# Three of four column groups of y transposed by DMA instead of TensorE, and C's gates fetched right behind A's

## The chip, the cores and the metric

The kernel runs on one NeuronCore of one Trainium2 chip. The metric is the device time of one execution in microseconds (us). Before the change the median of three runs is 1486.85 us (1486.48 to 1486.9). Engines are named as in the profile: PE is TensorE, DVE is VectorE, ACT is ScalarE, POOL is GpSimd, SP is SyncE, which here only issues DMAs.

## The reference

One decoder layer with three token mixers side by side, on 512 tokens and 2048 channels in float32. What matters here is the end of it:

```python
ua = (ya * silu(za)) @ w_branch_a          # sliding-window attention, 768 wide
ub = (yb * silu(zb)) @ w_branch_b          # forgetting attention, 768 wide
uc = (yc * silu(zc)) @ w_branch_c          # attention into memory tokens, 512 wide
g = sigmoid(gate_logits.reshape(b, s, 3, 2048))
y = g[:, :, 0] * ua + g[:, :, 1] * ub + g[:, :, 2] * uc
return x + y @ w_out
```

`y` is computed with tokens on partitions. For `y @ w_out` it is needed with channels on partitions, so y is transposed.

## The kernel before, in words

**Precision.** Every float32 product runs as three matmuls of a high and a low part: high x high, low x high, high x low. So each weights tile takes an ACT cast to the high part (`ac.copy`) and a DVE subtraction that leaves the low part. `parts` does both; in the profile the casts are at L1000 and L1125, the subtractions at L1001 and L1128.

**The late stage.** After the attention and z stages the kernel computes the three merge gates (stored to DRAM as `gates`), then y, then the product with w_out. A list of units, `late.units`, holds the order. y is made in four column groups (cg 0 to 3) of 512 channels. Each group has three units of branch B, three of A and two of C (class `Branch`), each of 24 matmuls of 128x512. DVE multiplies a finished bank by its gate (L1393 for B, which starts y; L1396 for A and C). POOL adds A's result to y, DVE adds C's.

**The transpose.** When C's last block is done, `flip` transposes the group: two pairs, each of eight 128x128 PE transposes into two PSUM banks (`yt`, L1421). The product with w_out uses seven block products in place of eight (a Strassen-like scheme), so `out` copies the four quarters of a pair into the places 3 and 4 (`y3s`, `y4s`, ACT L1430), makes four sums on DVE (L1012, L1015), stores one half of the results to DRAM (`y_alpha`, SP L1438, groups 0 to 2) and splits the other half into high and low (`yhy`, `yly`). `plan_y` later loads `y_alpha` back (`ya`, L1408), from the end of group 3's B units on, and splits it (`xhy`, `xly`).

**Places.** `place(n, ...)` are nine 4 KB-per-partition buffers, reused under many names. y lives in 5 and 7. Gates rotate through a ring of four (0, 1, 2, 6), two tiles per branch and group, so C's gates take the tiles of B's, and A's of the next group take those of C.

**What sets the order.** PE, DVE, ACT and POOL execute in the order that the program writes. That order comes from a clock that advances by 0.5 for every three matmuls; `later(dt, f)` puts f's instructions into their engines' streams dt further on. So one unit of 24 matmuls is 4 on this clock. The order on SP's queue is set by the framework's scheduler. Every engine and SP's queue run in order: an instruction that waits holds up all behind it. Weights for a unit are asked for four units ahead (`load`) and split two units ahead (`split`).

Of the kernel before, what the change touches and what calls it, by code (L numbers as in the profile page):

```python
# [11 lines left out]

F32 = mybir.dt.float32
F32R = mybir.dt.float32r
AF = mybir.ActivationFunctionType
ALU = mybir.AluOpType
AX = mybir.AxisListType
# [2 lines left out]
P = 128  # L20
# [36 lines left out]
def tile_hybrid_block(ctx, tc, xT, x, memT, mem, ng, mng, w_in, b_forget, gqa, gka, sinks, gqb, gkb, gqc, gkc,  # L57
                      w_mem, w_a, w_b, w_c, w_out, relm, out):
    nc = tc.nc
    ve, ac, po, pe, sy = nc.vector, nc.scalar, nc.gpsimd, nc.tensor, nc.sync  # L60
# [7 lines left out]
    def f32(ap):  # L68
        return ap.bitcast(F32)
# [9 lines left out]
    def place(n, name, dtype=F32):  # L79

        return yp.tile([P, 2, S], dtype, tag=f"ys{n}", name=name)
# [47 lines left out]
    yad = nc.dram_tensor("y_alpha", (D // 2, 1024), F32, kind="Internal").ap()  # L129
# [12 lines left out]
    def later(dt, f):  # L142
        at_slot(clock[0] + dt, f)
# [41 lines left out]

    def w_tile(which, dtype=F32R):

# [34 lines left out]
    def bank(i, name):  # L222
        return ps.tile([P, 512], F32, tag=TAGS[i], name=name)

    class Stream:
# [8 lines left out]
        def add(self, name, segs, kind, act, nkt, evac, pre=None):  # L234
            banks = {}
            nu = nkt if kind == "mem" else nkt // UK
            for u in range(nu):
                self.units.append((name, segs, kind, act, evac, pre, u, nu, banks))
# [756 lines left out]
    def blocks(xs):  # L995

        return xs.rearrange("p k (t n) -> p (k t) n", t=2)

    def parts(hi, lo, src, dt=0.5):
        ac.copy(hi, src)  # L1000
        later(dt, lambda: ve.tensor_tensor(lo, src, f32(hi), op=ALU.subtract))  # L1001

    def x_tiles(u, name):
        ax[u] = tuple(cp.tile([P, 4, 256], F32R, tag=f"a{p}{u}", name=f"x{p}{name}{u}") for p in "hl")
        return ax[u]

    def y_tiles(u, name):
        ay[u] = tuple(gp[0].tile([P, 3, 256], F32R, tag=f"b{p}{u}", name=f"y{p}{name}{u}") for p in "hl")
        return ay[u]
# [4 lines left out]
    def sub(out, a, b):  # L1014
        ve.tensor_tensor(out, a, b, op=ALU.subtract)  # L1015
# [50 lines left out]
    late = Late()  # L1066
# [248 lines left out]
    y_acc = {}  # L1315
# [19 lines left out]
    class Branch:  # L1335
# [20 lines left out]
        def fetch_g(self):  # L1356
            br, w, npair, gi, base = BR[self.bi]
            for i in range(2):
                t = r_tile(f"g{br}")
                sy.dma_start(out=t, in_=gdr[gi][i * 2 * P:(i + 1) * 2 * P, self.cg * 512:(self.cg + 1) * 512]  # L1360
                             .rearrange("(b p) n -> p b n", p=P))
                self.g[2 * i], self.g[2 * i + 1] = t[:, 0, :], t[:, 1, :]

        def run(self):
            br, w, npair, gi, base = BR[self.bi]
            xh, xl = y_split[base + self.p]
            first, last = self.p == 0, self.p == npair - 1
            if first:
                self.banks["tags"] = tags = ((2, 3), (0, 1))[ucnt[0] % 2]
                for b in range(4):  # L1370
                    self.banks[b] = bank(tags[b // 2], f"u{br}{self.cg}_{b}")
                ucnt[0] += 1
            if self.p == npair - 2:
                later(1, self.fetch_g)
            count = [0]
            for b in range(4):
                c = slice(b * P, (b + 1) * P)
                for k in range(2):
                    for i, (x, wt) in enumerate(((xh, self.hi), (xl, self.hi), (xh, self.lo))):
                        mm(count, self.banks[b], x[:, k, c], wt[:, k, :], start=(first and k == 0 and i == 0),  # L1380
                           stop=(last and k == 1 and i == 2))
                if last:
                    self.evac(b)
            if self.cg == 3 and last and self.bi == 0:
                plan_y()

        def evac(self, b):
            o, g = self.banks[b], self.g[b]
            if self.bi == 0:
                if b % 2 == 0:  # L1390
                    y_acc["t"] = place(5 + b, f"y{self.cg}{b}")
                y_acc[b] = y_acc["t"][:, b % 2, :]
                ve.tensor_tensor(y_acc[b], o, g, op=ALU.mult)  # L1393
                return
            y = y_acc[b]
            ve.tensor_tensor(g, o, g, op=ALU.mult)  # L1396
            if self.bi == 1:
                po.tensor_tensor(y, y, g, op=ALU.add)  # L1398
                return
            later(1, lambda: add(y, y, g))  # L1400
            if b == 3:
                flip(self.cg, dict(y_acc), self.banks["tags"])

    def plan_y():

        def one(u):
            xs = blocks(place(3 + u % 2, f"ya{u}"))
            sy.dma_start(out=xs, in_=yad[u * P:(u + 1) * P, :].rearrange("p (k n) -> p k n", n=256))  # L1408
            later(5, lambda: parts(*x_tiles(u, "y"), xs, 1))
        for u in range(6):  # L1410
            later((1, 3, 8, 10, 15, 17)[u], lambda u=u: one(u))

    def flip(cg, y, tags):

        def pair(q):
            u = 2 * cg + q
            banks = []
            for j in range(2):
                yt = bank(tags[q if cg < 3 else 1], f"yt{u}_{j}")
                for b in range(4):  # L1420
                    pe.transpose(yt[:, b * P:(b + 1) * P], y[b][:, (2 * q + j) * P:(2 * q + j + 1) * P], ident)  # L1421
                banks.append(yt)
            later(0.5, lambda: out(u, banks))

        def out(u, banks):
            xa, xb = (blocks(place(i, f"y{i}s{u}")) for i in (3, 4))
            a, s1, s2, d = (xa[:, i, :] for i in range(4))
            s3, c, s4, b = (xb[:, i, :] for i in range(4))
            for dst, j, h in ((b, 0, 1), (d, 1, 1), (a, 0, 0), (c, 1, 0)):
                ac.copy(dst, banks[j][:, h * 256:(h + 1) * 256])  # L1430

            def sums():
                add(s1, b, d)
                sub(s2, s1, a)
                sub(s3, a, b)
                sub(s4, c, s2)
                if cg < 3:
                    sy.dma_start(out=yad[u * P:(u + 1) * P, :].rearrange("p (k n) -> p k n", n=256), in_=xa)  # L1438
                parts(*y_tiles(u, "y"), xb[:, 0:3, :], 1)
                if cg == 3:  # L1440
                    later(2, lambda: parts(*x_tiles(u, "y"), xa, 1))
            later(1.5, sums)
        later(5, lambda: pair(0))
        later(9 if cg < 3 else 10.5, lambda: pair(1))

    for cg in range(4):
        for bi, (br, w, npair, gi, base) in enumerate(BR):
            banks, g = {}, {}
            for p in range(npair):
                late.units.append(Branch(cg, bi, p, banks, g))  # L1450
    n_branch = len(late.units)


# [73 lines left out]
    k = n_p4  # L1527
# [52 lines left out]
```

## Time and profile before

| | |
|---|---|
| median of three runs | 1486.85 us |
| the profiled execution's own time | 1487.16 us |
| its span | 1485.3 us |
| PE busy | 1476.7 us (99%) |
| DVE busy | 1086.1 us (73%) |
| ACT busy | 715.2 us (48%) |
| PE transposes of y | 64, first at 1197.4 us, last at 1342.6 us |
| column groups start at | 1190.73 (second), 1281.41 us (fourth) |

The profile shows one execution. Busy time is summed per engine. A group's row gives its count, busy time, the mean of one, and the idle time before it with what ended it. "The chain of waits" follows the last instruction back to what released it, step by step. Timeline rows begin with the start and the duration. Names are tiles: `rawl` raw weights, `wa` to `we` their high and low parts, `uA`, `uB`, `uC` the branches' banks, `P` the banks of a w_out product.

### The profile page before, as it was taken

The numbers are of one execution on the slowest core, as the hardware profiler recorded it, in microseconds if no ns is written. First come the engines' busy times: TensorE is split into PE (matmuls) and PEld (weight loads), VectorE is DVE, ScalarE is ACT, GpSimd is POOL, SyncE is SP. The second block draws the span as 40 slices with busy tenths as digits, with TensorE's granted clock in tenths as the row PEclk, the third lists the DMA queues.
The fourth block names the chain that finished last, engine by engine and source line by source line (L and its number), as shares of the span: only waits on it lengthen the run. The fifth ranks groups of instructions, "written<-read, shape, count | busy, mean of one in ns | idle before, by whom it ended". The sixth has DMA issues, their size and how long they took to land.

```text
span 1485.3 us, 20413 instructions
## 1 busy us (share of the span) xinstructions
PE 1476.7 (99%) x7225; PEld 1276.2 (86%) x7225; DVE 1086.1 (73%) x1868; ACT 715.2 (48%) x1206; POOL 202.8 (14%) x239
## 2 busy tenths in 40 slices
PE   9999999999999999999999999999999999999998
PEld 9999999998888888888888888888888888888887
DVE  5385875775678665469878888888887555589997
ACT  5545654664467564555344444444355332245442
POOL 0121431331334432200000000000000100110000
PEclk9999999999999999999999999999999999999999
DMA  8774235333345223476667676767676856476684
GB/s 287 223 214 127 79 94 160 88 108 120 122 140 164 74 87 98 161 256 233 202 219 226 216 224 213 239 205 245 209 228 214 294 179 207 162 247 222 245 285 154
DMA packets 127278, 277.40 MB, mean 187 GB/s; under 512 B 14140, under 2 KB 53692, under 8 KB 127176
## 3 DMA queue, kind: packets, MB, share of 16 engines
q1 hardware_dynamic: 122136, 259.58, 54.6%
q10 hardware_dynamic: 5040, 16.53, 3.3%
q8 instruction: 56, 0.92, 0.3%
q14 instruction: 46, 0.38, 0.1%
HBM read 244.58 MB, written 31.48 MB: 186 GB/s over the span
## 4 chain that ended last, share of the span: by engine, by line
PE 94%; ACT 2%; DMA 2%; DVE 1%; issue 1%; POOL 0%; ACTq 0%; DVEq 0%; POOLq 0%; SPq 0%
PE P L1083 41%; PE z L300 10%; PE qA L300 5%; PE kB L300 5%; PE vB L300 5%; PE qB L300 4%; PE uA L1083 4%; PE uB L1083 3%; PE qC L300 3%; PE kvA L300 3%; PE uC L1083 3%; PE mem L300 1%; PE avB L633 1%; PE ptB L623 1%; DMA gB<-gates 1%; PE avA L700 1%
## 5 line engine op out<-in xcount | busy, mean ns | idle before, releaser
L214 DVE TENSOR_TENSOR wc<-wa,wb 128x512 fp32r<-128x512 f32 (+2 forms) x254 | 149.7, 628 | 73.2 <-ACT wb L211 65.2
L211 ACT CAST wb<-wa 128x512 fp32r<-128x512 f32 (+2 forms) x254 | 131.4, 566 | 143.8 <-PE z L300 34.3
L1125 ACT CAST wa<-rawl 128x1024 fp32r<-128x1024 f32 x85 | 89.5, 1052 | 207.4 <-DVE rawl L1015 166.2
L1015 DVE TENSOR_TENSOR rawl<-rawl 128x512 f32<-128x512 f32 x256 | 176.9, 692 | 5.7 <-DMA rawl<-in_w_out_dram 1.3
L1128 DVE TENSOR_TENSOR wc<-rawl,wa 128x1024 fp32r<-128x1024 f32 x85 | 105.0, 1235 | 51.9 <-ACT wa L1125 50.3
L1128 DVE TENSOR_TENSOR we<-rawl,wd 128x512 fp32r<-128x512 f32 (+1 forms) x128 | 122.1, 954 | 4.1 <-ACT wd L1125 0.5
L1398 POOL TENSOR_TENSOR y<-y,gA 128x512 f32<-128x512 f32 x16 | 27.2, 1731 | 674.9 <-DVE gA L1396 674.9
L1125 ACT CAST wd<-rawl 128x512 fp32r<-128x512 f32 (+1 forms) x128 | 106.9, 835 | 22.7 <-DVE rawl L1015 19.9
L300 PE MATMUL z<-ah,wb 128*128 128x512 f32 x256 | 101.8, 398 | 0.0
L300 PE MATMUL z<-ah,wc 128*128 128x512 f32 x256 | 99.9, 390 | 0.0
L300 PE MATMUL z<-al,wb 128*128 128x512 f32 x256 | 99.8, 390 | 0.0
L1125 ACT CAST wb<-rawl 128x1024 fp32r<-128x1024 f32 x43 | 45.3, 1053 | 87.7 <-DVE rawl L1015 67.5
L1083 PE MATMUL P<-wd,xhx 128*128 128x512 f32 x192 | 74.7, 389 | 0.0
L1083 PE MATMUL P<-wd,xlx 128*128 128x512 f32 x192 | 74.7, 389 | 0.0
L1083 PE MATMUL P<-we,xhx 128*128 128x512 f32 x192 | 74.7, 389 | 0.0
L1128 DVE TENSOR_TENSOR wb<-rawl,wb 128x1024 fp32r<-128x1024 f32 x43 | 52.6, 1222 | 25.7 <-ACT wb L1125 25.4
L1012 DVE TENSOR_TENSOR R<-P,R 128x512 f32<-128x512 f32 (+1 forms) x90 | 57.1, 674 | 6.6 <-PE P L1083 5.8
L300 PEld LDWEIGHTS z<-ah,wc 128*128 128x128 f32 x256 | 48.0, 188 | 10.3
L300 PEld LDWEIGHTS z<-ah,wb 128*128 128x128 f32 x256 | 48.1, 188 | 9.3 <-DVE zA L937 0.3
L300 PEld LDWEIGHTS z<-al,wb 128*128 128x128 f32 x256 | 48.2, 188 | 9.1
L579 POOL TENSOR_SCALAR pA<-pA,denA 128x256 f32<-128x256 f32 (+1 forms) x48 | 45.0, 954 | 78.2 <-DVE denA L578 78.2
L1083 PE MATMUL P<-wa,xhx 128*128 128x512 f32 x128 | 49.8, 389 | 0.0
(407 smaller groups left out, 4189.6 us busy)
## 6 DMA issues: line engine op xcount, KB each, us to landing
rawl<-in_w_in_dram SPq DMA_DIRECT2D x144, 512.0 KB, 4.4
rawl<-in_w_out_dram SPq DMA_DIRECT2D x48, 512.0 KB, 5.7
wa<-in_w_in_dram SPq DMA_DIRECT2D x63, 384.0 KB, 3.5
wa<-in_w_in_dram SPq DMA_DIRECT2D x64, 256.0 KB, 3.0
rawl<-in_w_in_dram SPq DMA_DIRECT2D x48, 256.0 KB, 4.1
gates<-R ACTq DMA_DIRECT2D x24, 512.0 KB, 7.2
wa<-in_w_in_dram SPq DMA_DIRECT2D x16, 512.0 KB, 3.6
wa<-in_w_mem_dram SPq DMA_DIRECT2D x16, 512.0 KB, 3.4
```

The source lines that it names most:

```text
L211: ac.copy(hi[:, :n], raw[:, i, :n])
L214: ve.tensor_sub(lo[:, :n], raw[:, i, :n], f32(hi[:, :n]))
L300: pe.matmul(pb, a, m, start=b in fresh, stop=last and not todo[b])
L579: engine.tensor_scalar(p, p, den[:, 4 + i:5 + i], None, op0=ALU.mult)
L623: pe.transpose(tb[:, c:c + P], p[:, off[i] + j * P:off[i] + (j + 1) * P], ident)
L633: pe.matmul(av[:, j * P:], v[:, j, hv, :], t[:, BOFF[j]:BOFF[j] + n], start=(j == 0 and w == 0), stop=(j == NT - 1 and w == 1))
L1012: ve.tensor_tensor(out, a, b, op=ALU.add)
L1015: ve.tensor_tensor(out, a, b, op=ALU.subtract)
L1083: pe.matmul(*args, **kw)
L1125: ac.copy(hi[:, :k, :], src)
L1128: return lambda: ve.tensor_tensor(lo[:, :k, :], src, f32(hi[:, :k, :]), op=ALU.subtract)
L1398: po.tensor_tensor(y, y, g, op=ALU.add)
```

## The change

For column groups 0, 1 and 2 the PE transposes go. `flip_dma` does this in their place:

- `halves(b)`: ACT copies each token block of y, seen as 16-bit integers, into the tile of C's gates (whose use is over), low and high 16-bit halves apart. Four copies a group, of 1024 elements per partition.
- `send(h)`: SP issues a DMA transpose of a whole gates tile (128 partitions x 2048 16-bit elements, 512 KB) into y's own place, 5 or 7. Two a group.
- `combine`: as `out` before, but the copies (ACT, L1480 in the new numbering) read the transposed halves from SBUF and weave them back into 32-bit numbers: 512 16-bit elements each in place of 256 32-bit ones. The pairs are put at 6.5 and 8.5 on the clock behind the group's end (before, the copies were at 5.5 and 9.5).

Group 3 keeps the PE transposes. C's gates are asked for two clock steps behind A's, in A's second unit, and no longer in C's first. `plan_y` swaps the places 3 and 4 of the tiles that it loads. The ring of gates is unchanged.

```diff
@@ fetch_g
                 t = r_tile(f"g{br}")
                 sy.dma_start(out=t, in_=gdr[gi][i * 2 * P:(i + 1) * 2 * P, self.cg * 512:(self.cg + 1) * 512]
                              .rearrange("(b p) n -> p b n", p=P))
+                self.g["t", i] = t
                 self.g[2 * i], self.g[2 * i + 1] = t[:, 0, :], t[:, 1, :]
@@ Branch.run
-            if self.p == npair - 2:
+
+            if self.bi < 2 and self.p == npair - 2:
                 later(1, self.fetch_g)
+                if self.bi == 1:
+                    later(2, self.follower.fetch_g)
@@ Branch.evac
             if b == 3:
-                flip(self.cg, dict(y_acc), self.banks["tags"])
+                if self.cg < 3:
+                    flip_dma(self.cg, dict(y_acc), dict(self.g))
+                else:
+                    flip(self.cg, dict(y_acc), self.banks["tags"])
@@ plan_y
-            xs = blocks(place(3 + u % 2, f"ya{u}"))
+            xs = blocks(place(4 - u % 2, f"ya{u}"))
@@ 
+    def combine(u, copy):
+
+        cg = u // 2
+        xa, xb = (blocks(place(i, f"y{i}s{u}")) for i in (3, 4))
+        a, s1, s2, d = (xa[:, i, :] for i in range(4))
+        s3, c, s4, b = (xb[:, i, :] for i in range(4))
+        for dst, j, h in ((b, 0, 1), (d, 1, 1), (a, 0, 0), (c, 1, 0)):
+            copy(dst, j, h)
+
+        def sums():
+            add(s1, b, d)
+            sub(s2, s1, a)
+            sub(s3, a, b)
+            sub(s4, c, s2)
+            if cg < 3:
+                sy.dma_start(out=yad[u * P:(u + 1) * P, :].rearrange("p (k n) -> p k n", n=256), in_=xa)
+            parts(*y_tiles(u, "y"), xb[:, 0:3, :], 1)
+            if cg == 3:
+                later(2, lambda: parts(*x_tiles(u, "y"), xa, 1))
+        later(1.5, sums)
+
@@ flip
-                yt = bank(tags[q if cg < 3 else 1], f"yt{u}_{j}")
+                yt = bank(tags[1], f"yt{u}_{j}")
...
-            later(0.5, lambda: out(u, banks))
+            later(0.5, lambda: combine(u, lambda dst, j, h: ac.copy(dst, banks[j][:, h * 256:(h + 1) * 256])))
         later(5, lambda: pair(0))
-        later(9 if cg < 3 else 10.5, lambda: pair(1))
+        later(10.5, lambda: pair(1))
+
+    def u16(ap):
+        return ap.bitcast(U16)
+
+    def flip_dma(cg, y, g):
+        back = {}
+
+        def halves(b):
+            t = u16(g["t", b // 2]).rearrange("p i (x n) -> p (i x) n", n=P).rearrange("p (e k b) n -> p e k b n", e=2, b=2)
+            ac.copy(t[:, :, :, b % 2, :], u16(y[b]).rearrange("p (k n e) -> p e k n", k=4, e=2))
+
+        def send(h):
+            t = u16(place(5 + 2 * h, f"yh{cg}{h}"))
+            sy.dma_start_transpose(out=t.rearrange("p i (x n) -> p (i x) n", n=P),
+                                   in_=u16(g["t", h]).rearrange("p i n -> p (i n)"))
+            back[h] = t.rearrange("p i (k n) -> p i k n", k=4)
+
+        for h in range(2):
+            for b in (2 * h, 2 * h + 1):
+                later(0.5 + 0.5 * b, lambda b=b: halves(b))
+            later(1.5 + h, lambda h=h: send(h))
+        for q in range(2):
+            later((6.5, 8.5)[q], lambda q=q: combine(2 * cg + q, lambda dst, j, h: ac.copy(
+                u16(dst).rearrange("p (n e) -> p e n", e=2), back[h][:, :, 2 * q + j, :])))
@@ 
+            if bi == 2:
+                late.units[-4].follower = late.units[-2]
```

How the instructions move. First ACT at the border from group 0 to group 1, before (`rawl113` is the weights of A's second unit of group 1, `yt` the banks of PE's transposes):

```order
L1000 CAST wb127_11118<-rawl111_11030 128x1024 [waits DMAHW2_49,DVE_49,PE_49]
L1000 CAST wd102_11158<-rawl112_11068 128x1024 [waits DMAHW5_49,DVE_49,PE_49]
L1430 COPY y4s0_11169<-yt0_0_11148 128x256 [waits PE_49]
L1430 COPY y3s0_11168<-yt0_1_11153 128x256 [waits PE_49]
L1430 COPY y3s0_11168<-yt0_0_11148 128x256
L1430 COPY y4s0_11169<-yt0_1_11153 128x256
L1000 CAST yhy0_11189<-y4s0_11169 128x768 [waits DVE_49]
L1000 CAST wa127_11217<-rawl113_11105 128x1024 [waits DMAHW6_49]
L1430 COPY y4s1_11226<-yt1_0_11207 128x256 [waits DVE_49,PE_49]
L1430 COPY y3s1_11225<-yt1_1_11212 128x256 [waits DMAHW3_49,PE_49]
L1430 COPY y3s1_11225<-yt1_0_11207 128x256
L1430 COPY y4s1_11226<-yt1_1_11212 128x256
```

After the change ACT's stream at the same place reads so (`gC` the gates' tiles that take the halves, `yh` the transposed ones):

```order
L1467 COPY gC_30_10980<-y02_10907 128x8x128
L1001 CAST wd102_11156<-rawl112_11068 128x1024 [waits DMAHW5_49,PE_49,Activation_49]
L1480 COPY y4s0_11174<-yh01_11137 128x2x256 [waits DMAHW1_49,Activation_49]
L1480 COPY y3s0_11173<-yh01_11137 128x2x256
L1480 COPY y3s0_11173<-yh00_11126 128x2x256 [waits DMAHW7_49]
L1480 COPY y4s0_11174<-yh00_11126 128x2x256
L1001 CAST yhy0_11193<-y4s0_11174 128x768 [waits DVE_49]
L1480 COPY y4s1_11202<-yh01_11137 128x2x256 [waits DVE_49]
L1480 COPY y3s1_11201<-yh01_11137 128x2x256 [waits DMAHW5_49]
L1480 COPY y3s1_11201<-yh00_11126 128x2x256
L1480 COPY y4s1_11202<-yh00_11126 128x2x256
L1001 CAST wa127_11211<-rawl113_11105 128x1024 [waits DMAHW6_49,PE_49]
```

The copies of halves have come in between the weights casts (the last one is the first row); the cast of `rawl113` stood between the two pairs and now stands behind the second. The four copies of a pair read `yh`, and the second copy of the second pair waits for a DMA, the store of what the first pair left in that place.

DVE at the same border, after the change (`wc127` is the low half of `rawl113`, `y10` the next group's y):

```order
L1013 TENSOR_TENSOR y3s0_11173<-y4s0_11174,y3s0_11173 128x256 [waits Activation_49]
L1016 TENSOR_TENSOR y3s0_11173<-y3s0_11173 128x256 [waits DVE_49,Activation_49]
L1016 TENSOR_TENSOR y4s0_11174<-y3s0_11173,y4s0_11174 128x256
L1016 TENSOR_TENSOR y4s0_11174<-y4s0_11174,y3s0_11173 128x256 [waits DVE_49,Activation_49]
L1002 TENSOR_TENSOR yly0_11194<-y4s0_11174,yhy0_11193 128x768 [waits Activation_49]
L1398 TENSOR_TENSOR y10_11214<-uB1_0_11107,gB_31_11159 128x512 [waits DMAHW3_49,DMAHW7_49,PE_49,Activation_49]
L1013 TENSOR_TENSOR y3s1_11201<-y4s1_11202,y3s1_11201 128x256 [waits DMAHW5_49]
L1016 TENSOR_TENSOR y3s1_11201<-y3s1_11201 128x256 [waits DVE_49]
L1016 TENSOR_TENSOR y4s1_11202<-y3s1_11201,y4s1_11202 128x256
L1016 TENSOR_TENSOR y4s1_11202<-y4s1_11202,y3s1_11201 128x256 [waits DVE_49]
L1002 TENSOR_TENSOR wc127_11212<-rawl113_11105,wa127_11211 128x1024 [waits DMAHW6_49,Activation_49]
```

Before, `wc127` stood directly behind the multiply that writes `y10`, ahead of the second pair's sums; now it is behind them. The multiply also waits for ACT now: `y10` lies where the transposed halves are read.

SP's queue at this border, before:

```order
L1342 DMA rawl113_11105<-in_w_a_dram 128x2x512 [waits DMAHW6_49,DMAHW1_49,DVE_49]
L1360 DMA gA_33_11305<-gates_0 128x2x512 [waits DVE_49]
L1360 DMA gA_34_11307<-gates_0 128x2x512 [waits DMAHW0_49,DVE_49]
L1342 DMA rawl114_11140<-in_w_a_dram 128x2x512 [waits DMAHW2_49,DVE_49]
L1342 DMA rawl115_11199<-in_w_c_dram 128x2x512 [waits DMAHW5_49,DVE_49]
L1438 DMA y_alpha<-y3s0_11168 128x1024 [waits DMAHW3_49,DVE_49]
L1342 DMA rawl116_11260<-in_w_c_dram 128x2x512 [waits DMAHW6_49,DMAHW4_49,DVE_49]
L1438 DMA y_alpha<-y3s1_11225 128x1024 [waits DVE_49]
```

and after:

```order
L1343 DMA rawl113_11105<-in_w_a_dram 128x2x512 [waits DMAHW6_49,DMAHW1_49,DVE_49]
L1471 DMA_TRANSPOSE yh00_11126<-gC_29_10978 128x16x128 [waits DVE_49,Activation_49]
L1343 DMA rawl114_11148<-in_w_a_dram 128x2x512 [waits DMAHW2_49,DMAHW0_49,DVE_49]
L1471 DMA_TRANSPOSE yh01_11137<-gC_30_10980 128x16x128 [waits Activation_49]
L1343 DMA rawl115_11196<-in_w_c_dram 128x2x512 [waits DMAHW5_49,DVE_49]
L1361 DMA gA_33_11293<-gates_0 128x2x512 [waits DMAHW7_49,DMAHW3_49]
L1361 DMA gA_34_11295<-gates_0 128x2x512 [waits DMAHW4_49,DMAHW1_49]
L1436 DMA y_alpha<-y3s0_11173 128x1024 [waits DVE_49]
L1436 DMA y_alpha<-y3s1_11201 128x1024 [waits DMAHW6_49,DVE_49,Activation_49]
L1343 DMA rawl116_11248<-in_w_c_dram 128x2x512 [waits DVE_49]
```

The next group's A gates have moved from ahead of one weights transfer to behind two, and behind both transposes; the two stores of `y_alpha` now stand together, ahead of the weights of C's second unit (`rawl116`). In group 3 the first request for `ya` (L1408, new L1416) stands for place 4 in place of 3, and the transfers of the second w_out unit (`rawl134`) stand behind `ya2` instead of ahead of it.

More of the change, by code (lines that the diff above doesn't have):

```diff
@@ L14 @@
 F32R = mybir.dt.float32r
+U16 = mybir.dt.uint16
 AF = mybir.ActivationFunctionType
@@ L1422, in pair @@
                 banks.append(yt)
-            later(0.5, lambda: out(u, banks))
[L1425 to L1442, printed above, removed]
-        later(5, lambda: pair(0))
-        later(9 if cg < 3 else 10.5, lambda: pair(1))
+            later(0.5, lambda: combine(u, lambda dst, j, h: ac.copy(dst, banks[j][:, h * 256:(h + 1) * 256])))
+        later(5, lambda: pair(0))
+        later(10.5, lambda: pair(1))
[18 more added lines that the diff above has]
+                u16(dst).rearrange("p (n e) -> p e n", e=2), back[h][:, :, 2 * q + j, :])))
     for cg in range(4):
```

## Prediction

> **What bounds the kernel now.** I read the busy shares first, then who PE waits for, then busy time by stretch for the stage that changes (1190 to 1346 us: three column groups and their borders) and the one behind it.
>
> ```profile
> span 1485.3 us, 20413 instructions
> PE 1476.7 (99%) x7225; PEld 1276.2 (86%) x7225; DVE 1086.1 (73%) x1868; ACT 715.2 (48%) x1206; POOL 202.8 (14%) x239
> ...
> PE uA L1083 <- DVE wb L1001: 0.2, 1, 0.2
> ...
> 1209.00:1236.00 27.00, 27.00 (x121) 22.36 (x120) 13.44 (x17) 7.50 (x8) 6.94 (x4) 1.00 0.57 191
> ...
> 1309.00:1346.00 37.00, 37.00 (x173) 30.80 (x172) 35.38 (x44) 19.82 (x29) 6.41 (x4) 1.00 0.64 219
> 1346.00:1400.00 54.00, 54.00 (x240) 44.72 (x239) 50.42 (x62) 26.49 (x30) 0.00 (x0) 1.00 0.74 258
> ```
>
> PE bounds the time: it is busy for 99% of the span, and in this stage waits for nothing longer than the 0.2 us shown. In a stretch stand its length and then PE, PEld, DVE, ACT and POOL busy. Inside the column groups both are about half idle (DVE 13.44 of 27 us). Behind them, from 1309 us, DVE has 35.38 of 37 us and then 50.42 of 54. So work taken off PE shortens the first stretch directly, but in the second DVE has to follow.
>
> **What is removed.** The chain of waits, in order of time, is PE alone here:
>
> ```profile
> 1190.73 6.81 PE uB L1083 x30
> 1197.54 0.87 PE yt L1421 x8
> 1198.42 5.49 PE uB L1083 x24
> 1203.90 0.88 PE yt L1421 x8
> 1204.78 4.09 PE uB L1083 x18
> 1208.87 16.32 PE uA L1083 x72
> 1225.19 10.88 PE uC L1083 x48
> ...
> 1281.41 6.81 PE uB L1083 x30
> ```
>
> Eight transposes (yt, L1421) take 0.87 to 0.88 us of PE's time. Groups 0, 1 and 2 have two such packets each: 6 x 0.88 = **-5.3 us**. That is all that can be gained. Matmuls follow each other at 10.88/48 = 0.227 us.
>
> **What is added, at each of three borders.** I count t from a column group's first B matmul (t = 0 is 1190.73). The unit after B's three and A's first is A's second; it starts at 96 x 0.227 = 21.8 and needs the low half of its weights at its third matmul, t = 22.2. In the changed order the cast of these weights (wa from rawl113) stands on ACT behind the second pair's copies, and their low half (wc) on DVE behind the second pair's four sums; before, both stood ahead of that pair. So the new route must end by 22.2. Its durations, first from the timeline (start, duration), then three rows of groups (mean or median ns of one):
>
> ```profile
> 1189.82 0.69 DVE L1012 TENSOR_TENSOR y<-y,gC 128x512 f32<-128x512 f32 x1
> ...
> 1192.62 0.69 DVE L1012 TENSOR_TENSOR y<-y,gC 128x512 f32<-128x512 f32 x1
> 1193.23 1.22 DVE L1001 TENSOR_TENSOR wb<-rawl,wb 128x1024 fp32r<-128x1024 f32 x1
> 1194.47 0.37 SPq L1342 DMA_DIRECT2D rawl<-in_w_a_dram  x1
> ...
> 1198.86 0.43 DVE L1012 TENSOR_TENSOR y3s<-y4s,y3s 128x256 f32<-128x256 f32 x1 [3.27 <-ACT y3s L1430]
> 1200.07 0.42 DVE L1015 TENSOR_TENSOR y4s<-y4s,y3s 128x256 f32<-128x256 f32 x1
> 1200.52 0.84 ACT L1000 CAST yhy<-y4s 128x768 fp32r<-128x768 f32 x1 [1.14 <-DVE y4s L1015]
> 1201.39 0.96 DVE L1001 TENSOR_TENSOR yly<-y4s,yhy 128x768 fp32r<-128x768 f32 x1 [0.90 <-ACT yhy L1000]
> 1209.33 1.04 ACT L1000 CAST wd<-rawl 128x1024 fp32r<-128x1024 f32 x1
> 1210.27 1.05 ACT L1000 CAST wa<-rawl 128x1024 fp32r<-128x1024 f32 x1
> L211 ACT CAST wb<-wa 128x512 fp32r<-128x512 f32 (+2 forms) x254 | 131.4, 566 | 143.8 <-PE z L300 34.3
> L1125 ACT CAST wa<-rawl 128x1024 fp32r<-128x1024 f32 x85 | 89.5, 1052 | 207.4 <-DVE rawl L1015 166.2
> L1430 ACT COPY y3s<-yt x16: 372/379/392, 1198.5 to 1344.2; 128x256 f32<-128x256 f32 x16
> ```
>
> ACT first splits y into halves: a copy of 1024 16-bit elements, priced as the 1024-element cast, 1.05 us, the next 0.95 behind it (1209.33, 1210.27). No copy of 16-bit integers is in this trace; per element the two casts shown agree, so I take that rate, with half of it and double as bounds (-2 to +4 us on the route). The first two follow the second block's add (ends 1190.51, t = -0.2); then comes one weights cast; the last two end at 4.6, later than the last add (1193.31, t = 2.6). On SP one weights transfer stands between the transposes, and waits for a low half of 1.22 us that ends about 4.0; so the second transpose is asked for at about 4.7 and lands at X = 4.7 + L.
>
> From X: two copies of 512 elements (0.57, a second 0.47 later) and two sums put the store of y_alpha at X + 2.0. It lands 3.9 later, X + 5.9; the other two sums, the cast of 0.84 and its low half (0.96) end earlier, at X + 4.6. The second pair rewrites the stored place, so three of its copies start at X + 5.9 and end at X + 7.4. Then DVE's queue: one multiply of B's output (0.69; it writes where the halves came back, so it waits for these copies, and everything behind it on DVE too), four sums (1.6), the low half (1.22): X + 10.9. PE stalls when X > 11.3, that is **L > 6.6 us**, from there 1 us per us and border.
>
> The price of L, the landing of a 512 KB transpose, isn't in this trace. The nearest rows are plain transfers of that size (last figure: median us to landing; the first row is y_alpha's store):
>
> ```profile
> DMA to landing us min/median/max: 2.6/3.9/4.1
> ...
> gA<-gates SPq DMA_DIRECT2D x8, 512.0 KB, 4.7
> gC<-gates SPq DMA_DIRECT2D x8, 512.0 KB, 5.6
> yC<-ys_C SPq DMA_DIRECT2D x2, 512.0 KB, 9.0
> ya<-y_alpha SPq DMA_DIRECT2D x6, 512.0 KB, 5.7
> ```
>
> Bounds: 2.6, and 9.0 where a transfer queues behind others. A weights transfer of the same size is asked for 0.3 us ahead, so I take gA's 4.7 and 1.3 more: **L = 6.0**, X = 10.7. The route then ends 0.6 us before PE needs it: cost 0 with a thin margin. At 9.0 it is 3 x 2.4 = +7.2. [...]
>
> The rest costs nothing. ACT gets 12 half copies (12.6 us) and 24 copies of 0.57 in place of 0.38 (4.5), in stretches with 7.50 of 27 us busy; uncovered, they would delay weights casts one for one. A's gates move on SP behind both transposes, C's behind the next weights: asked for at about X + 11 = 22 and needed at 39, landing in 5.6. That weights transfer (rawl116) leaves at the same time and is needed at 38.1.
>
> **Behind the last group.** Here DVE is nearly full, and its work starts with y_alpha coming back:
>
> ```profile
> 1301.12 1.84 SPq L1408 DMA_DIRECT2D ya<-y_alpha  x2
> 1304.21 0.70 SPq L1103 DMA_DIRECT2D rawl<-in_w_out_dram  x1
> ...
> 1308.44 2.00 ACT L1000 CAST xhy<-ya 128x1024 fp32r<-128x1024 f32 x2 [6.44 <-DMA ya<-y_alpha]
> 1309.53 2.36 DVE L1001 TENSOR_TENSOR xly<-ya,xhy 128x1024 fp32r<-128x1024 f32 x2 [5.56 <-ACT xhy L1000]
> 1331.48 0.69 DVE L1012 TENSOR_TENSOR y<-y,gC 128x512 f32<-128x512 f32 x1
> 1333.40 1.04 PE L1421 MATMUL yt<-ident,y 128*128 128x128 f32 x8
> ```
>
> In the last group's own clock (t = 0 at 1281.41) ya is asked for at 19.7 now. After the change its place is free when the second pair's low half is done, X + 12.4 = 23.1; with 5.7 to land and a cast, DVE's block starts at 29.9, not 28.1: 1.8 us later. PE, without two packets, reaches group 3's first remaining transposes 1.8 us earlier in that clock, at 50.2; the last add that they need ends at 1332.17, t = 50.8, and would now end at 52.6. Of the 1.6 us that DVE idles in 1309 to 1346, I give back 0.6: a stall of **+1.8 us**. Behind it PE would be 3.5 us earlier than now, DVE's work 2.3 (two borders' 3.5, less 1.8, plus 0.6); of the missing 1.2 us I charge half, since DVE has 3.6 idle us in the next 54: **+0.6**. And the transfers of the second w_out unit, asked for at 1304.21 now, fall behind ya2 on SP, so ACT's casts come later: bounds 0 and 2, taken **+0.8**.
>
> Sum, from the profiled execution's 1487.16 us (its span and 1.86 around it): 1487.16 - 5.3 + 0 + 1.8 + 0.6 + 0.8 = 1485.1. The median of the runs is 0.31 lower: **1484.8 us**. A measurement of this kernel can't tell 0.2% (3.0 us) from no change; 2.1 is inside it.
>
> **Rivals.**
> - The gain arrives whole. For it: 1.6 and 3.6 idle us on DVE, matmuls that now end earlier, a landing near 2.6 to 3.9. Against: 35.38 of 37 us busy. 1486.85 - 5.3 = 1481.5. Chance 0.22.
> - The transposes land late, and PE waits in every group for A's second unit, through ACT's blocked copies and DVE's blocked multiply. At L = 9.0: -5.3 + 7.2 + 3.2 (the tail's terms) + 0.6 (ya later by 3.0, of which PE's own 2.4 are paid already) = +5.7, 1492.5; slower by more than 0.2% from L = 8.1. [...] Against: medians of 3.9 to 5.7. Chance 0.24.
> - The sixteen 128x128 blocks of a transpose go one after another, with L at twice the longest row, 18: 3 x 11.4 = 34, less 5.3 and plus 3.8: 1519. No row speaks for it. Chance 0.03. [...]
> - It doesn't do what it says: the gates' places tie A's gates to the transposes, and nothing moves earlier. They are needed at 28.5 and would land at X + 6; 1487. Chance 0.03.
>
> **How the numbers follow.** The forecast, between 1482.5 and 1488, has 0.48. Faster by over 0.2%: the first rival and the forecast's lower edge (0.06), 0.28. Slower: the late landings and the blocks, 0.27. The same: 0.45. The range, 1481.6 to 1495.5, leaves out the lowest whole gains and landings beyond L = 10.
>
> **What will show it.** 16 transposes on PE, 0.227 us between matmuls across each border. In ACT's groups, the first copy of a pair waits for the transpose, and the second pair's for the store: L is issue to landing of L1471's DMA. If PE waits show DVE's wc or wd (L1002) at uA, L was above 6.6; if they show yt waiting for y, or P for w_out halves, it is the tail. No PE wait at all, and 5 us less, would prove the tail's terms wrong; L above 8 the forecast.

## The result, and the profile after

Median of six runs after: 1492.4 us (1490.75 to 1492.65); before, on the same chip, 1486.8 (1486.48 to 1486.95). The ratio is 1.0035 (95% interval 1.0025 to 1.0045): **slower, by 5.6 us**. The forecast was 1484.8, a gain of 2.1 us that the prediction itself counted as no measurable change. The profiled execution after took 1490.75 us, the fastest of the six, so its trace accounts for 3.6 of the 5.6 us (before: 1487.16); the other 2.0 us, from it to the median, no trace shows.

The page's head and its waits of PE, after:

```profile
span 1489.0 us, 20351 instructions
...
PE 1474.2 (99%) x7177; PEld 1271.7 (85%) x7177; DVE 1086.1 (73%) x1868; ACT 734.7 (49%) x1218; POOL 204.8 (14%) x239
```

```profile
PE uA L1084 <- DVE wc L1002: 2.7, 2, 1.7
...
PE P L1084 <- DVE gC L1401: 1.9, 2, 1.1
PE uA L1084 <- DVE wb L1002: 1.4, 1, 1.4
...
PE uA L1084 <- ACT wa L1001: 0.2, 1, 0.2
```

PE is still the engine with 99%, and its busy time fell by 2.5 us only, although 48 transposes are gone; around the waits below its matmuls run more slowly (at the first border 0.33 us from one to the next, where 0.227 is usual). It has new waits in two places. At each of the three borders it waits for the weights of A's second unit (`uA` for `wc`, `wb`, `wa`), 4.3 us in all; before, PE's one such wait, 0.2 us, lay ahead of these groups. At the start of w_out it waits for DVE's multiplication of C (`P` for `gC`), 1.9 us; before, there was none.

**The borders.** From group 1's first B matmul to the first matmul of w_out PE took 136.02 us before (1190.57 to 1326.59) and 136.08 after (1190.15 to 1326.23). So the three borders took back all of the 5.3 us that the six packets of transposes had cost. The three units of A, 72 matmuls, lasted 16.3 us per group before and 18.8, 17.6 and 18.1 after, 5.5 us more in all: the 4.3 us of waits, and 1.2 us around them, where matmuls follow each other more slowly (0.33 us from the one at 1214.65 to the next; 0.227 is usual). The chain of waits at the first border (start, duration) is no longer PE alone:

```profile
1194.99 6.71 DMA yh<-gC
...
1201.77 0.77 ACT y4s L1480
1202.55 1.26 ACT y3s L1480 x2
...
1204.29 4.93 DMA y_alpha<-y3s
...
1209.88 0.76 ACT y3s L1480
1210.64 0.64 ACT y4s L1480
...
1211.30 0.69 DVE y L1398
...
1213.46 1.15 DVE wc L1002
...
1214.65 1.43 PE uA L1084 x5
```

It reads as the prediction's route does, with longer steps: the second transpose lands 6.7 us after it was asked for (X = 1201.70), the first pair's copies and sums take 2.6, the store of `y_alpha` 4.9, then come the second pair's copies, B's multiplication, the four sums and the low half, at X + 12.9.

**The end.** From w_out's first matmul to the end of the span it is 158.7 us before (1326.59 to 1485.3) and 162.8 after (1326.23 to 1489.0): 4.1 us, all of the profiled loss. In time order there, from the timeline, first before and then after:

```profile
1324.75 0.68 DVE L1396 TENSOR_TENSOR gC<-uC,gC 128x512 f32<-128x512 f32 x1
...
1326.59 0.39 PE L1083 MATMUL P<-wa,yhy 128*128 128x512 f32 x1
```

```profile
1312.96 1.05 ACT L1001 CAST xhy<-ya 128x1024 fp32r<-128x1024 f32 x1 [6.56 <-DMA ya<-y_alpha]
...
1314.04 2.46 DVE L1002 TENSOR_TENSOR xly<-ya,xhy 128x1024 fp32r<-128x1024 f32 x2 [4.39 <-ACT xhy L1001]
...
1326.23 0.39 PE L1084 MATMUL P<-wa,yhy 128*128 128x512 f32 x1
...
1329.37 0.68 DVE L1401 TENSOR_TENSOR gC<-uC,gC 128x512 f32<-128x512 f32 x1
...
1330.20 0.47 PE L1084 MATMUL P<-wd,yhy 128*128 128x512 f32 x1 [1.09 <-DVE gC L1401]
```

DVE's block on the rows of `y_alpha` starts at 1314.04 and not at 1309.53. DVE's first multiplication of C, 1324.75 before, is at 1329.37, 3.1 us behind w_out's first matmul instead of 1.8 ahead of it. C's banks are emptied late, and PE waits for one.

### The profile page after: what moved, and what is told of

Read it like the earlier page. It is cut to its first block, busy times and chain, and to the rows that moved or that the text cites. A ratio compares the mean times of both kernels' runs of the same rounds, so it can differ in the third digit from the quotient of the medians.

```text
span 1489.0 us, 20351 instructions
## 1 busy us (share of the span) xinstructions
PE 1474.2 (99%) x7177; PEld 1271.7 (85%) x7177; DVE 1086.1 (73%) x1868; ACT 734.7 (49%) x1218; POOL 204.8 (14%) x239
## 4 chain that ended last, share of the span: by engine, by line
PE 89%; ACT 3%; DVE 3%; DMA 3%; issue 2%; POOL 0%; DVEq 0%; ACTq 0%; POOLq 0%
PE P L1084 41%; PE z L301 10%; PE qA L301 5%; PE kB L301 5%; PE vB L301 5%; PE qB L301 4%; PE uA L1084 3%; PE qC L301 3%; PE kvA L301 3%; PE mem L301 1%; PE uC L1084 1%; DMA yh<-gC 1%; PE uB L1084 1%; DMA y_alpha<-y3s 1%; PE avB L634 1%
## 5 line engine op out<-in xcount | busy, mean ns | idle before, releaser
L1126 ACT CAST wd<-rawl 128x512 fp32r<-128x512 f32 (+1 forms) x128 | 106.8, 835 | 23.1 <-DVE rawl L1016 20.7
L608 POOL TENSOR_SCALAR biB<-cb,cq 128x128 f32<-128x128 f32 (+3 forms) x48 | 34.5, 718 | 112.8 <-DVE denB L599 97.2
```

The source lines that it names most:

```text
L608: po.tensor_scalar(bi[:, :n], kv()[5][:, :n], -1.0, cq[:, i, h:h + 1], op0=ALU.mult, op1=ALU.add)
L1126: ac.copy(hi[:, :k, :], src)
```

## The experiments

Group 3 goes by PE in all of them. Two moments of each profiled execution carry the reading: when PE starts w_out (P, the first row of that product), and when DVE starts its first multiplication of C in group 3 (gC). The last column is explained below the table. Every interval is against the kernel before, on the same chip.

| kernel | median, us | ratio, 95% | P | gC | span | larger of P + 158.7 and gC + 159.6 |
|---|---|---|---|---|---|---|
| before | 1486.8 | | 1326.59 | 1324.75 | 1485.3 | 1485.3 |
| the change | 1492.4 | 1.0025 to 1.0045 | 1326.23 | 1329.37 | 1489.0 | 1489.0 |
| e1_gates | 1486.95 | 0.9991 to 1.0009 | 1326.43 | 1324.59 | 1485.2 | 1485.1 |
| e2_group0 | 1487.57 | 0.9998 to 1.0016 | 1326.68 | 1324.84 | 1485.3 | 1485.4 |
| e3_group2 | 1491.35 | 1.0018 to 1.0040 | 1325.99 | 1329.08 | 1488.7 | 1488.7 |
| e5_three_split | 1490.7 | 1.0016 to 1.0037 | 1324.17 | 1329.58 | 1489.0 | 1489.2 |
| e6_three_low | 1486.25 | 0.9987 to 1.0005 | 1321.54 | 1324.43 | 1484.0 | 1484.0 |
| e7_two_low | 1483.73 | 0.9970 to 0.9988 | 1323.57 | 1321.74 | 1482.1 | 1482.3 |
| e8_own_place | 1487.04 | 0.9992 to 1.0010 | 1324.60 | 1326.89 | 1486.3 | 1486.5 |
| e9_own_ya | 1485.47 | 0.9981 to 0.9999 | 1323.37 | 1324.78 | 1484.6 | 1484.4 |
| e12_ya_behind | 1490.81 | 1.0016 to 1.0039 | 1328.15 | 1329.44 | 1488.8 | 1489.0 |
| e13_low_behind | 1484.86 | 0.9983 to 1.0002 | 1321.14 | 1323.62 | 1483.0 | 1483.2 |
| e10_own_ya_low | 1485.53 | 0.9984 to 1.0002 | 1320.65 | 1323.39 | 1483.0 | 1483.0 |
| e11_dose | 1495.36 | 1.0048 to 1.0074 | 1331.85 | 1333.25 | 1492.8 | 1492.9 |

158.7 is the kernel before's own time from P to the end. 159.6 was read off the runs in which gC comes behind P, and then the larger of the two sums gives every span within 0.2 us. So the end has two possible owners. Where gC comes well ahead of P (1.8 us in four kernels), it is PE, and the route at the borders decides. Where gC comes behind P (by 1.3 us and more in the other ten), it is DVE, and PE's start no longer matters: P differs by 2.1 us between e5 and the change, and the span is the same. The two sums cross at a lead of 0.9 us; that is worked out and not measured, since no kernel lies between 1.8 us ahead and 1.3 behind. In e5, e6 and e10 PE waits behind P also for the cast of the rows of `y_alpha` (`xhy`: 3.4, 0.8 and 0.7 us; in e5 for nothing else); the sum fits there too.

The lateness of gC is made early. In twelve of these kernels DVE's first multiplication of C comes 12.9 us behind its first of A in group 3 (`gA`), whether both are early or late. So what counts is what holds A's multiplication up, and that is the block on the rows of `y_alpha` ahead of it in DVE's queue. The other two are e12 and e13, which move that block.

My theory when the runs began: each border's stall is the route, which puts the low half of A's second unit behind the second pair of y; the loss behind the last group is group 2's late pair, through the rows of `y_alpha` and DVE's queue. Rivals: the new order of gates and places; the transposes' traffic, which would slow other transfers.

### The new order without the transposes: e1

```diff
-                if self.cg < 3:
+                if self.cg < 0:
                     flip_dma(self.cg, dict(y_acc), dict(self.g))
-                yt = bank(tags[1], f"yt{u}_{j}")
+                yt = bank(tags[q if cg < 3 else 1], f"yt{u}_{j}")
-        later(10.5, lambda: pair(1))
+        later(9 if cg < 3 else 10.5, lambda: pair(1))
```

> C's gates are asked for early and the two places of y are swapped, as in the change, but all four column groups are transposed by TensorE as before. Route theory (the loss comes from what stands behind the DMA route of y: a stall of 1.0 to 1.9 us at A's second unit at each border, and a late block of VectorE behind the last group): no route, so 1486.8 within 0.5, no wait of PE on the low half of A's second unit, granted clock 1.00 at the start of w_out. Order theory (the early gates and the swapped places hold SP's and VectorE's queues up): the loss is here already, 1488.5 to 1492.5. Traffic theory (the transposes and their 16-bit packets slow the other transfers): 1486.8, since there are none.

1486.95 us, ratio 1.0 (0.9991 to 1.0009). C's early gates and the swapped places cost nothing by themselves. The order theory falls.

### One group alone: e2 (group 0) and e3 (group 2)

As e1, with `self.cg == 0` and `self.cg == 2` for the condition.

> As in the change, but only group 0 goes by DMA; groups 1, 2 and 3 by TensorE. Route theory: 1.76 us of transposes removed, 1.7 us of stall at group 1's second A unit put in their place, nothing behind the last group: 1486.8 (1486.2 to 1487.4), with one wait of PE on the low half and a granted clock of 1.00 at the start of w_out. A rival in which each group by DMA loses the same, a third of the 5.6 us: 1488.7.

> As in the change, but only group 2 goes by DMA. Route theory: 1.76 us removed, 1.5 us of stall at group 3's second A unit, and the whole loss behind the last group (two waits of PE on the C multiplication and some 3.7 us at a clock near 0.6, together about 4 us): 1490.5 (1489.5 to 1491.5). The rival in which each group loses the same: 1488.7. Order or traffic theory: between 1487 and 1489, and the clock stays at 1.00.

e2 1487.57, e3 1491.35. In e2 PE's one new wait from 1180 us on is the border's, 1.7 us, and takes back the 1.76 us of two packets; P to the end is as before. e3's waits from 1180 us on:

```profile
PE P L1084 <- DVE gC L1401: 1.8, 2, 1.0
PE uA L1084 <- DVE wb L1002: 1.0, 1, 1.0
PE yt L1450 <- DVE y L1013: 0.9, 1, 0.9
```

One group by DMA, and the whole loss behind the last group is there: gC 1329.08, as in the change. It belongs to group 2, the one whose pairs come just ahead of the rows of `y_alpha`, and is no sum over groups. e2's eleven runs were seven from 1486.7 to 1488.0 and four from 1489.2 to 1489.9, which the expectation did not have; a possible reason stands in the last section.

### The weights ahead of the second pair: e5, e6 and e7

e5 moves the cast (ACT) and the low half (DVE) of A's second unit earlier on the clock:

```diff
+    for cg in (1, 2, 3):
+        late.units[n_gates + 8 * cg + 2].when = (0.5, 0, 3.5, 0.25)
```

e6 moves the low half also ahead of B's first multiplication:

```diff
+    for cg in (1, 2, 3):
+        late.units[n_gates + 8 * cg + 2].when = (0.5, 0, 3.5, 0.5)
...
-            parts(self.hi, self.lo, self.raw[:, 0:2, :], 1)
+            parts(self.hi, self.lo, self.raw[:, 0:2, :], dt)
```

e7 is e6 with `cg in (1, 2)`, and with e1's edit so that groups 0 and 1 alone go by DMA (`self.cg < 2`).

> The change with one thing moved: the cast and the low half of A's second unit stand ahead of the copies and sums of the second pair of y on ScalarE and VectorE, in groups 1, 2 and 3. Route theory: the three stalls of 1.0 to 1.9 us at A's second unit are gone (5 us), the route itself ends no earlier, by up to 1 us later, so the loss behind the last group (4 us) stays or grows by a microsecond: 1487.5 (1485.5 to 1489). If it is the traffic or SP's queue that makes the low half late, moving it ahead changes nothing: 1491.5 to 1492.5.

1490.7 us: above the range that I gave. The timeline of DVE shows why:

```profile
1211.80 0.69 DVE L1398 TENSOR_TENSOR y<-uB,gB 128x512 f32<-128x512 f32 x1 [5.03 <-ACT y4s L1480]
1212.40 1.22 DVE L1002 TENSOR_TENSOR wc<-rawl,wa 128x1024 fp32r<-128x1024 f32 x1
```

B's first multiplication writes y's own place, where the halves came back, so it waits 5.03 us for the last copy out of it, and the low half stands behind it. Its cast had been done since 1206.7. Two of the three stalls stayed (1.0 and 1.2 us).

> As the run before with the second A unit's cast moved ahead, but its low half now also stands ahead of B's first multiplication on VectorE (that one waits for the last copy out of the places in which the halves came back, 5 us). Route theory: no wait of PE on a low half of A in any of the three groups, so the 5.3 us of the transposes are kept up to the start of w_out, and the loss behind the last group (3 to 5 us) is all that is left: 1486.5 (1485 to 1489). If traffic delays the weights themselves, PE still waits there: 1489 or more.

1486.25 us (expected 1486.5). DVE at the same place:

```profile
1207.39 1.23 DVE L1002 TENSOR_TENSOR wc<-rawl,wa 128x1024 fp32r<-128x1024 f32 x1
1211.60 0.69 DVE L1398 TENSOR_TENSOR y<-uB,gB 128x512 f32<-128x512 f32 x1 [2.99 <-ACT y4s L1480]
```

PE has no wait left in the three borders. Its windows (length, then PE busy) are full up to w_out, with the transposes' traffic still there (DMA share 0.72 and 0.85):

```profile
1190.00:1236.00 46.00, 46.00 (x205) 38.09 (x204) 27.71 (x39) 20.39 (x24) 5.91 (x4) 1.00 0.72 217
1236.00:1281.00 45.00, 45.00 (x201) 37.24 (x200) 25.91 (x37) 20.34 (x25) 6.90 (x4) 1.00 0.72 210
1281.00:1321.00 40.00, 40.00 (x178) 33.14 (x177) 24.50 (x30) 19.42 (x23) 7.44 (x4) 1.00 0.85 256
```

Group 1's first matmul to P is 130.56 us here, 5.5 less than in the change. That shows what the border stalls were: the place of one cast and one low half behind the second pair, in two queues. No transfer had to become faster, so weights that traffic makes late aren't it.

> Groups 0 and 1 by DMA, group 2 by TensorE again, and A's second unit cast and subtracted ahead of the second pair and of B's first multiplication. Route theory: four packets of transposes gone (3.5 us), no wait at A's second unit, nothing late behind the last group: 1483.5 (1483 to 1484.5), faster than both. If transposes by DMA cost the other transfers something, 1485 to 1487.

**1483.73 us, ratio 0.9979 (0.9970 to 0.9988): better than both.** One wait of 0.5 us is left at a border. Behind the last group DVE is ahead of PE as in the kernel before:

```profile
1321.74 0.68 DVE L1401 TENSOR_TENSOR gC<-uC,gC 128x512 f32<-128x512 f32 x1
```

### The second pair's own place, and where the rows come back: e8 and e9

```diff
-       xa, xb = (blocks(place(i, f"y{i}s{u}")) for i in (3, 4))
+       xa = blocks(place(3, f"y3s{u}") if own is None else own)
+       xb = blocks(place(4, f"y4s{u}"))
```

`own` is the tile of C's gates that the first transpose has read (`g["t", 0]`), given for the second pair only. e9 also loads `ya` into `place(3 + u % 2)` again.

> The change, but the second pair's stored sums get a place of their own (the tile of C's gates that the first transpose has read), so its copies no longer wait for the first pair's store of y_alpha to land; nothing else is moved. Route theory: the 1.6 us of that wait leave the route in every group, the stalls at A's second unit shrink from 1.0 to 1.9 us to 0 to 0.4, and the rows of y_alpha are asked for 1.6 us earlier behind the last group, where the loss falls from 4 us to about 2: 1484.5 (1483 to 1487). Traffic theory: the store and the transposes take as long as before, 1490 to 1492.

> As the run with a place of its own for the second pair, and the first rows of y_alpha come back into the place that the first pair leaves free, as in the kernel before, and not into the one that the second pair's low half holds. Route theory: these rows are asked for at t of about 20 and no longer 25, VectorE's block behind the last group starts where it started before (1309.5 us) or earlier, and no loss is left there: 1482 (1481.5 to 1484). If the loss there is the clock's or the transposes' traffic, 1485 or more.

e8 1487.04, e9 1485.47: both some 2.5 to 3.5 us above what I expected, and e9 in the region (1485 or more) that its expectation gives to the clock or the traffic. The clock is not it: PE's granted clock is 1.00 in e9 from 1186 to 1360 us. ACT in e8 no longer waits for the store (the change has 1.64 us before its copies at 1209.24):

```profile
1208.32 0.78 ACT L1481 COPY y4s<-yh 128x512 uint16<-128x512 uint16 x1 [1.02 <-DVE yly L1002]
1208.96 1.39 ACT L1481 COPY gC<-yh 128x512 uint16<-128x512 uint16 x2
```

The pair's copies end 19.6 us behind the group's first matmul (1191.33), in the change 21.1. But 0.6 to 1.1 us of a stall stayed at two borders, and gC came only partly back: it lies 47.3 us behind group 3's first B matmul in e8 and 46.0 in e9, after 48.4 in the change, against 43.5 in the kernel before and in e7. e9's DVE shows what is left:

```profile
1306.72 1.22 DVE L1002 TENSOR_TENSOR xly<-ya,xhy 128x1024 fp32r<-128x1024 f32 x1
1310.70 1.23 DVE L1002 TENSOR_TENSOR xly<-ya,xhy 128x1024 fp32r<-128x1024 f32 x1 [2.75 <-ACT xhy L1001]
```

The first rows' block starts 27.9 us into the group, as early as expected (28.3 in the kernel before). But the second rows go to place 4, and are asked for at 1303.37 (24.6 us into the group; 21.4 before), when the second pair's low half has left it. DVE waits 2.75 us for their cast, and A's first multiplication comes 2.5 us later in the group than before. That is all of what gC lost.

### The rows behind A's multiplications: e12 and e13

```diff
-            later(5, lambda: parts(*x_tiles(u, "y"), xs, 1))
+            later(9 if u < 2 else 5, lambda: parts(*x_tiles(u, "y"), xs, 1))
```

e13 is this together with e6.

> The change with the first two casts and low halves of y_alpha's rows placed 4 steps later, behind A's first two multiplications of group 3 on ScalarE and VectorE; the borders are left as they are. Route theory: VectorE no longer holds A's and C's multiplications behind rows that land late, so the two waits of PE for C's multiplication (1.9 us) and the slow clock behind them (1.8 us) shrink or go: 1489.5 (1488 to 1491). If VectorE is simply full there, or the loss follows the rows and not their place in the queue: 1491.5 to 1493.

> Three groups by DMA with both repairs that worked alone: A's second unit cast and subtracted ahead of the second pair and of B's first multiplication, and the first two rows of y_alpha cast behind A's first two multiplications of group 3. Route theory with repairs that add up: w_out starts 5.4 us earlier than in the kernel before, and the stretch behind it is longer by the 1.9 us that the second repair left alone: 1483.5 (1482.5 to 1484.5). If a PE that arrives earlier meets a VectorE that is busy without a pause there, the stretch behind the last group takes back 3 to 4 us, as without the second repair: 1485 to 1487.

e12 1490.81, inside the range I gave, but its interval overlaps the change's: no difference shown by the time. In the profile gC is 46.6 us behind group 3's first matmul (the change 48.4), and P to the end 160.7 (162.8); PE lost those 2 us again at a border, in the clock (last section). A's first multiplication is as early as in the kernel before (30.5 us into the group), but the block now stands between A's and C's, 16.1 us apart. e13 1484.86, between the two theories' ranges: with the stalls gone PE reaches w_out 5.5 us earlier than before, and gC 1.1. DVE takes back 3.2 us of what PE gained (the span is 2.3 us shorter). Two windows of e13 (length, PE, PEld, DVE busy):

```profile
1320.00:1330.00 10.00, 8.79 (x39) 6.61 (x37) 9.87 (x15) 5.05 (x7) 0.00 (x0) 1.00 0.76 259
1330.00:1340.00 10.00, 9.11 (x48) 7.54 (x47) 9.90 (x15) 6.18 (x11) 0.00 (x0) 1.00 0.43 142
```

### All repairs together: e10

e6, e8 and e9 in one.

> All three repairs together, with three groups by DMA: a place of its own for the second pair's sums, the first rows of y_alpha back in the free place, and A's second unit cast and subtracted ahead of the second pair. Route theory: no wait of PE at A's second unit; what stays behind the last group is what VectorE, 35 of 37 us busy there, cannot do sooner for a PE that arrives 5 us earlier (0.9 to 1.5 us at group 3's transposes): 1482.7 (1481.7 to 1484.2), faster than the two-group kernel by about 1. If the third group by DMA is worth nothing because VectorE bounds that stretch: 1483.5 to 1485.

1485.53, not 1482.7: the rival in the expectation, that the third group by DMA is worth nothing, is nearer. The rows of `y_alpha` are early now, and DVE waits for something else:

```profile
1307.04 1.23 DVE L1002 TENSOR_TENSOR xly<-ya,xhy 128x1024 fp32r<-128x1024 f32 x1 [1.75 <-ACT xhy L1001]
1310.54 0.69 DVE L1401 TENSOR_TENSOR gA<-uA,gA 128x512 f32<-128x512 f32 x1 [2.27 <-DMA gA<-gates]
```

A's gates arrive 2.27 us late, because one of their two places now holds the pair's sums until its store is done. In every kernel with group 2 by DMA gC comes 46.0 to 50.7 us behind group 3's first matmul. What the best order there would reach isn't settled.

### A longer route: e11

```diff
+            for _ in range(2 if b > 1 else 1):
                 ac.copy(t[:, :, :, b % 2, :], u16(y[b]).rearrange("p (k n e) -> p e k n", k=4, e=2))
```

> The change with the last two half copies of each group made twice, so that the second transpose of each group is asked for about 1.9 us later (two 16-bit copies of 0.95 apart); nothing else is added. Route theory: each stall at A's second unit grows by 1.9 us (to 2.9 to 3.8), 5.7 in all, and the rows of y_alpha behind the last group do not come later than these stalls make PE: 1498 (1495.5 to 1500.5). If the route's end were not what PE waits for, less than 1 us: 1491.5 to 1493.5.

1495.36, below the range of the route theory, above the other's: not a clean dose. The scheduler answered it by putting one load of A's gates ahead of the second transpose on SP:

```profile
1195.63 0.37 SPq L1361 DMA_DIRECT2D gA<-gates  x1
1196.80 4.41 SPq L1472 DMA_TRANSPOSE yh<-gC  x1
...
1203.39 0.37 SPq L1361 DMA_DIRECT2D gA<-gates  x1
1205.91 7.11 SPq L1436 DMA_DIRECT2D y_alpha<-y3s  x2
```

So at the first border X came 1.6 us later, but the store landed in 3.1 us and no longer in 4.9, and the second pair, which waits for the store, ended where it had. The waits at the borders grew by 2.2 us in all. The way from group 1 to w_out grew by 6.0, though; the larger part of that is a halved clock behind the waits at the second and third border (0.50 from 1262 to 1264 us and from 1310 to 1312).

## Why the prediction was wrong, point by point

- **The removal, -5.3:** right. With the stalls gone (e6) group 1 to w_out is 5.5 us shorter.
- **The border at 0, "the route then ends 0.6 us before PE needs it":** this step failed, and it turned the sign: taken as 0 at three borders, measured as 5.4 us. The threshold of 6.6 for L was wrong, more than L itself, which was 6.7, 6.2 and 6.8 against the 6.0 taken; at the second border PE waited 1.0 us with L below it. At the first border the route from X to the low half was 12.9 us and not 10.9, so that the threshold in the prediction's own sum was 4.6. Its terms: copies and sums before the store 2.6 (taken 2.0), since two copies of 16-bit elements started 0.65 apart and took 0.77 each, where I had scaled a cast (0.57, 0.47 apart); the store 4.9 (3.9); three more such copies and a gap (2.1 against 1.5).

```profile
L1480 ACT COPY y4s<-yh x12: 758/770/778, 1201.8 to 1300.6; 128x512 uint16<-128x512 uint16 x12
...
L1471 SPq DMA_TRANSPOSE yh<-gC x6: 1598/2898/4683, 1192.1 to 1285.8; - x6
```

  The copy of 1024 elements into halves was as priced (1.04 us): a rate per element carried over for one shape and not for the other.
- **"The rest costs nothing":** wrong for A's gates. The prediction moves them behind both transposes and charges nothing for that. SP asked for them even ahead of X, in front of the store:

```profile
1199.77 0.53 SPq L1343 DMA_DIRECT2D rawl<-in_w_c_dram  x1
1200.40 1.68 SPq L1361 DMA_DIRECT2D gA<-gates  x2
1204.29 8.90 SPq L1436 DMA_DIRECT2D y_alpha<-y3s  x2
```

  With both loads just ahead, the first pair's store landed in 4.2 to 5.5 us (19 borders in eight kernels, the change's 4.9, 4.4 and 4.3 among them); where one of them had been moved off, in 3.1 to 3.8 (the 12 borders of e8 to e11). None of these runs varies this alone, so the difference of about 1 us is a reading and not a test. C's gates, forecast at X + 11 = 22, were asked for 25.1 us into the group, and no engine waited for them there.
- **The rival that happened** is "the transposes land late, and PE waits in every group for A's second unit, through ACT's blocked copies and DVE's blocked multiply". Mechanism and place were right (e6 shows it), its chance of 0.24 was too low, and its condition (L = 8.1) was not needed. That its 1492.5 is nearly the 1492.4 measured is luck: it has 7.2 us at the borders for an L of 9.0, and the profiled execution 5.4 for 6.2 to 6.8.
- **Behind the last group, +3.2 in three terms:** the direction was right, the size 0.9 short and the accounting wrong. Rows asked for 25 us into the group and not 23.1, 6.7 to land and not 5.7: DVE's block began at 33.1, not 29.9. The largest term, +1.8 for a stall of PE at group 3's transposes, did not come there: in the change PE waits for nothing at them, but 1.9 us for gC at the start of w_out, which the prediction does not name. The lateness was charged in parts, half here, half there; in the runs the larger of P + 158.7 and gC + 159.6 gives the end. In the change the second is the larger, by 4.0.
- **The slow clock there** (granted 0.57 and 0.58 from 1332 to 1336 us) looked like a cost of its own. The change's windows (the number before the last two is the granted clock):

```profile
1330.00:1332.00 2.00, 1.02 (x4) 0.57 (x4) 1.90 (x5) 0.02 (x1) 0.00 (x0) 1.00 0.99 352
1332.00:1334.00 2.00, 2.00 (x6) 1.57 (x7) 2.00 (x4) 0.00 (x0) 0.00 (x0) 0.57 0.92 283
1334.00:1336.00 2.00, 2.00 (x7) 1.57 (x6) 2.00 (x3) 1.98 (x3) 0.00 (x0) 0.58 0.44 170
```

  But e3 has the same lateness of gC behind P (3.1 us), the clock at 1.00 throughout, and nearly the same time from P to the end, 162.7 us (162.8). Behind the last group the slow matmuls ran in time that PE would have waited for DVE.
- **The blocks in series, at an L of 18:** excluded. In the change a transpose of sixteen 128x128 blocks landed in 3.6 to 6.8 us, so at most 0.43 per block. The loads of the same size of gA and gC in the kernel before took 4.7 and 5.6 us (medians).
- **The sum:** in the profiled execution 1487.16 - 0.4 (group 1 started that much earlier) - 5.3 + 5.4 at the borders + 4.1 at the end = 1491.0, measured 1490.75. The forecast had 0 and 3.2 for the last two terms. The 2.0 us from there to the median are in no term.

## What to carry to other kernels

Work taken off the bounding engine is worth what the next queue leaves of it: before pricing the removal, find for each following stage the second engine's first instruction that the first engine needs, and its lead (here 1.8 us, DVE ahead of PE at w_out; by estimate from the two sums above 0.9 of it could be spent). When a step becomes a longer route through other engines, list what stands behind its waiting instructions on each of them, and move what another engine needs soon ahead of it; here two rows moved (e6) turned +5.6 us into no loss, and two groups in place of three into a gain of 3.2. A result that returns into its source's own place ties the next writer of that place, and all behind it in its queue, to the last reader (in e5 B's first multiplication on DVE waited 5.03 us for ACT's last copy, and the low half behind it, whose cast had been done since 1206.7, started at 1212.40).

## What the runs showed of the hardware

- **PE's granted clock halved behind short waits at some borders.** It fell to 0.50 for about 3.5 us behind two waits of 0.4 and 1.7 us that ended 2.4 us apart, here e12's first border:

```profile
1214.00:1216.00 2.00, 1.22 (x3) 1.02 (x4) 2.00 (x3) 2.00 (x3) 0.00 (x0) 0.67 0.60 228
1216.00:1218.00 2.00, 2.00 (x7) 1.52 (x6) 2.00 (x4) 0.42 (x1) 0.00 (x0) 0.50 0.86 262
```

  The branch took 20.5 us from first to last matmul there: 16.3 without a wait, 2.1 of waits, 2.1 more. Nearly the same waits (0.3 and 1.7) at e11's first border left it at 1.00; what decides between the two is not shown. By estimate from the 2.1 us at e12's border, two executions of one kernel could differ by some 2 us. e2's two clusters lie 2.4 us apart, and its four longer executions have a mean granted clock of 0.998, the seven shorter ones 0.999 or 1.000; that fits such a fall, but only one of the shorter ones has a trace. The change's six executions don't sort that way (1490.75 us at 0.999, 1492.32 at 1.000), so the 2.0 us between its profiled execution and its median stay open.
- **A transpose held its issuing queue.** In the change SP was held 1.6 to 4.7 us per 512 KB transpose (the row of L1471 above), where a load of that size takes 0.3 to 0.6 there; the second one of a pair landed in 6.2 to 6.8 us, the first in 3.6 to 3.8.
